# Second FFN: nine of ten blocks by seven products instead of eight, with forty plain units at five or four places of each block's steps

## The chip, the cores and the metric

The kernel runs on one core of a Trainium2 chip. The metric is the device time of one execution in microseconds (us). Three executions of the kernel before took 2602.81, 2605.07 and 2609.3 us; the median is 2605.07 us.

## The reference

One layer of a diffusion backbone with 256 context and 256 latent tokens of width 2048: a half-step SwiGLU FFN, a mixer (attention beside a bidirectional mLSTM), and a second half-step SwiGLU FFN, each behind an RMS norm with modulation by a condition vector. The change is in the second FFN, which works on the 256 latent tokens alone:

```python
def half_step_ffn(x, mod, i, g, w_up, w_down):
    h = adaln(x, g, mod, i)
    a, b = jnp.split(h @ w_up, 2, axis=-1)
    return x + 0.5 * mod[:, i + 2, None, :] * ((jax.nn.silu(a) * b) @ w_down)
...
        xl = half_step_ffn(xl, mod_l, 6, g_norm[l, 2], w_ffn2_up[l], w_ffn2_down[l])
...
    return rms_norm(xl, g_final)
```

`h` is 256 x 2048, `w_up` 2048 x 11264 (a half of 5632 columns for `a` and one for `b`), `w_down` 5632 x 2048, all in float32.

## The kernel before, in words

**Precision.** A float32 operand is split into a high part `hi` (written by ACT, line 127, rounded to the matmul's format) and the rest `lo` (by DVE, line 128). A product is made of three matmuls, hi x hi, hi x lo and lo x hi (`mm3`, lines 149 to 151). `split` does this for a weight tile of 128 x 2048 (1 MB) in two halves of 1024 columns; the `hi` and `lo` halves lie in four slots each, so a split can run at most four halves ahead of TensorE. `load_split` loads a tile into one of three `raw` slots through SP's queue (line 142) and splits it.

**Blocks.** The 5632 hidden columns are 44 groups of 128, and the second FFN takes them as eleven blocks of 512, numbers 0 to 10. Block 0 is made ahead, in the stage before. For each other block, the kernel multiplies the tokens by the block's 512 columns of `a` and of `b` (the up product), gates (`silu(a) * b`), turns the result by transposes on TensorE so that hidden columns lie on the partitions, splits it (`turned`, lines 2041 to 2062), and multiplies by the block's 512 rows of `w_down` into an accumulator `acc2`.

**Two ways to make an up product.** `up(n)` is the plain one: eight units, each loads one 1 MB tile and runs 4 x 2 x 3 = 24 matmuls of 128 x 128 by 128 x 512 (four chunks of 128 features, two halves of the tokens). `quad(n)` is a scheme with seven products in place of eight: tokens are cut in two halves and features in two halves, and the two weight halves of `a` and the two of `b` are the four parts of the other factor. Seven combinations of the token quarters (`a11`, `a12`, `a21`, `a22` and the sums `n1`, `s4`, `s2`, `s3`, built once by `token_forms`) are multiplied with seven combinations of the weight parts. Products are called m0 to m6 here, after the loop variable in `quad`; each is two steps (`q` = 0 and 1), and a step splits one 1 MB weight tile and runs 12 matmuls, into the PSUM tile X or Y. Fourteen steps have 168 matmuls, where eight plain units have 192.

**How the weight combinations come about.** Two pairs of 1 MB tiles, `weights[0]` (tags `c0` and `c1`, called chain in the profile) and `weights[1]` (called ra) change roles from block to block: one is `chain_`, the other `ra`. `chain_` is loaded plainly by SP while the block before runs (`again`, in m5, line 2121); after the split of m0 POOL adds the next part of the weights onto it with an accumulating DMA (`accum`, line 730, called by `first`), for m2; after the split of m2 DVE adds the `ra` tile to it (`summed_half`, line 2077), for m4; after the split of m4 a further accumulating DMA (`chained(0, 2)`), for m6. `ra` is loaded plainly in m0 (line 2130), read in m3, and takes an accumulating DMA for m5. m1 reads a plain load into a `raw` slot (`plain`, line 2125). Each accumulating DMA waits for the `lo` part of the split before it, on POOL's queue, and the split of the later product waits for its landing. A block by seven products so has six plain and six accumulating loads of 1 MB, a plain one eight plain loads.

**The order.** `sequence` (lines 2241 to 2249) names the order of two streams: "s" is a step of the blocks by seven products, in the order of `QUADS`; "u" is a plain unit, in the order of `units`. Plain units are the eight of an `up(n)`, and those of the down products: `down(n, n + 1)` runs eight units, each with one 1 MB load (line 142) and 24 matmuls, and adds the pair's result to `acc2`. Behind the two steps of m0 no unit stands; behind m1 to m6 one stands each, save behind m3 in the fourth and the eighth block of `QUADS`. After each "s" or "u" `turned` is called, which turns the next finished block half in the order of the block numbers; it needs one of three hid tiles (`N_HID`), which come free when a pair's down product is summed. After the sequence come the tail: `down(8, 9)` and block 10's down product with the final gate, residual and norm. `before_final` loads the gate and the final gain into the tags `c0` and `c1`, the tiles of `weights[0]`.

The program's text gives priorities and dependencies; a planner writes the list of each engine and each DMA queue from them, in order of its own estimate of when an instruction can run. An engine runs its list in order.

## Time and profile before

| | us |
|---|---|
| median of three executions | 2605.07 |
| lowest, highest | 2602.81, 2609.3 |
| the profiled execution's own time | 2604.58 |
| its span in the profile | 2602.7 |
| second FFN's sequence of steps and units, from the first plain unit to the tail | 1949.61 to 2525.90 of the span |
| tail (down products of blocks 8 to 10, norm, output) | 2525.90 to 2602.70 of the span |

The profile is of one execution. PE is TensorE's matmuls, PEld its weight loads, DVE the vector engine, ACT the scalar engine, POOL the GpSimd engine (here it issues accumulating DMAs), SP the engine that issues plain DMAs. Matmuls overlap one another, so the duration in a matmul's row (0.39 us) is longer than the distance to the next one's start. In a row of a single instruction the columns are its start, its duration, engine, line, operation, the tiles it writes and reads, and in brackets the engine's idle time before it and what ended it. For a DMA issue, the duration is that of issuing; the time to landing is told by the view of DMA issues. `hi<-raw`, `hi<-chain` and `hi<-ra` are splits of a raw slot and of the two pairs of weight tiles.

### The profile page before, as it was taken

The page shows a single profiled execution, that of the slowest core. Times are in us where ns is not written, and L with a number is a line of the kernel's source. Part 1 is how long each engine was busy: PE and PEld are TensorE (multiplying, and loading weights), DVE is VectorE, ACT ScalarE, POOL GpSimd, SP SyncE. Part 2 cuts the span into 40 slices and gives each one's busy share as a digit, 9 for nine tenths or more (in the row PEclk, how much of TensorE's full clock was granted, in tenths as well). Part 3 has the DMA queues.
Part 4 walks back from the last instruction along what each step waited for, and adds up shares of the span by engine and source line. Part 5 has one row for each costly group of instructions (what it writes and reads, how often), then busy time and mean ns, then how long its engine had stood idle before and what let it go on. Part 6 is the DMA issues. An engine that isn't in the chain of part 4 may idle for free.

```text
span 2602.7 us, 33781 instructions
## 1 busy us (share of the span) xinstructions
PE 2575.7 (99%) x12670; PEld 2144.7 (82%) x12670; DVE 2170.6 (83%) x2864; ACT 1417.7 (54%) x1810; POOL 220.7 (8%) x269
## 2 busy tenths in 40 slices
PE   8999999999999999999999999999999999999998
PEld 5788888888888888888889889888897888888887
DVE  7788888878888788888887889798889878887887
ACT  4454444544444565444454347456476676666664
POOL 0000000100000100000110000120000000000001
PEclk8999999999999999999999999999999999999999
DMA  9889999999999988889987887776768988999876
GB/s 392 350 217 265 276 277 271 262 273 285 261 287 265 278 247 240 218 215 228 225 253 266 296 312 247 242 273 213 267 239 240 269 269 260 272 273 279 256 231 176
DMA packets 127219, 681.01 MB, mean 262 GB/s; under 512 B 14152, under 2 KB 16712, under 8 KB 64976
## 3 DMA queue, kind: packets, MB, share of 16 engines
q1 hardware_dynamic: 98544, 493.25, 50.7%
q0 software_dynamic: 28512, 185.61, 36.4%
q8 instruction: 99, 1.62, 0.2%
q14 instruction: 64, 0.52, 0.1%
HBM read 660.91 MB, written 17.89 MB: 261 GB/s over the span
## 4 chain that ended last, share of the span: by engine, by line
PE 85%; DVE 7%; DMA 5%; issue 2%; ACT 1%; POOL 0%; ACTq 0%; POOLq 0%; SPq 0%; DVEq 0%
PE mm L151 21%; PE mm L150 21%; PE mm L149 21%; DVE lo L128 2%; PE mm L87 2%; PE Y L149 2%; PE Y L151 2%; PE Y L150 2%; PE X L151 2%; PE X L150 2%; PE X L149 2%; PE tr L150 1%; PE tr L149 1%; PE tr L151 1%; PE tr L87 1%
## 5 line engine op out<-in xcount | busy, mean ns | idle before, releaser
L127 ACT ACTIVATE hi<-raw 128x1024 fp32r<-128x1024 f32 (+2 forms) x500 | 517.8, 1041 | 421.1 <-PE mm L151 264.1
L128 DVE TENSOR_TENSOR lo<-raw,hi 128x1024 fp32r<-128x1024 f32 (+2 forms) x488 | 583.6, 1207 | 149.7 <-ACT hi L127 130.5
L127 ACT ACTIVATE hi<-chain 128x1024 fp32r<-128x1024 f32 x336 | 355.0, 1059 | 305.7 <-PE mm L151 188.0
L128 DVE TENSOR_TENSOR lo<-chain,hi 128x1024 fp32r<-128x1024 f32 x336 | 407.2, 1221 | 118.0 <-ACT hi L127 114.3
L149 PE MATMUL mm<-hi,hhi 128*128 128x512 f32 (+3 forms) x1024 | 393.6, 385 | 0.0
L151 PE MATMUL mm<-hi,hlo 128*128 128x512 f32 (+3 forms) x1024 | 386.7, 378 | 0.0
L150 PE MATMUL mm<-lo,hhi 128*128 128x512 f32 (+3 forms) x1024 | 386.7, 378 | 0.0
L207 DVE SCALAR_TENSOR_TENSOR junk<-sraw,cBh 128x1024 fp8e5<-128x1024 f32 x192 | 234.3, 1220 | 19.2 <-DMA sraw<-in_w_mt 16.7
L151 PEld LDWEIGHTS mm<-hi,hlo 128*128 128x128 f32 x1024 | 192.5, 188 | 33.9
L149 PEld LDWEIGHTS mm<-hi,hhi 128*128 128x128 f32 x1024 | 192.6, 188 | 31.0
L150 PEld LDWEIGHTS mm<-lo,hhi 128*128 128x128 f32 x1024 | 192.8, 188 | 30.7
L128 DVE TENSOR_TENSOR lo<-ra,hi 128x1024 fp32r<-128x1024 f32 x96 | 117.0, 1223 | 39.7 <-ACT hi L127 35.8
L127 ACT ACTIVATE hi<-ra 128x1024 fp32r<-128x1024 f32 x96 | 101.9, 1061 | 65.1 <-PE mm L151 48.4
L149 PE MATMUL mm<-hi,hid2h 128*128 128x512 f32 x352 | 137.1, 390 | 0.0
L151 PE MATMUL mm<-hi,hid2l 128*128 128x512 f32 x352 | 137.0, 389 | 0.0
L150 PE MATMUL mm<-lo,hid2h 128*128 128x512 f32 x352 | 136.9, 389 | 0.0
L207 DVE SCALAR_TENSOR_TENSOR sr<-sr,cBl 128x1024 f32<-128x1024 f32 x84 | 103.0, 1234 | 14.7 <-DMA sr<-in_w_mt 13.8
L730 POOL DMA_DIRECT2D chain<-in_w_up1b x60 | 53.1, 886 | 726.0 <-DVE lo L128 648.9
L149 PE MATMUL mm<-hhi,hi 128*128 128x512 f32 (+1 forms) x288 | 101.4, 352 | 0.0
L151 PE MATMUL mm<-hhi,lo 128*128 128x512 f32 (+1 forms) x288 | 99.0, 344 | 0.0
L150 PE MATMUL mm<-hlo,hi 128*128 128x512 f32 (+1 forms) x288 | 98.7, 343 | 0.0
L149 PE MATMUL mm<-hi,sumshl 128*128 128x512 f32 x200 | 77.8, 389 | 0.0
(517 smaller groups left out, 5650.3 us busy)
## 6 DMA issues: line engine op xcount, KB each, us to landing
raw<-in_w_dn SPq DMA_DIRECT2D x70, 1024.0 KB, 7.5
chain<-in_w_up1b POOLq DMA_DIRECT2D x60, 1024.0 KB, 9.8
sraw<-in_w_mt SPq DMA_DIRECT2D x96, 512.0 KB, 7.8
sr<-in_w_mt SPq DMA_DIRECT2D x81, 512.0 KB, 5.5
raw<-in_w_up1b SPq DMA_DIRECT2D x40, 1024.0 KB, 7.9
mraw<-in_w_m SPq DMA_DIRECT2D x32, 1024.0 KB, 7.4
raw<-in_w_up2b SPq DMA_DIRECT2D x32, 1024.0 KB, 9.9
chain<-in_w_dn POOLq DMA_DIRECT2D x30, 1024.0 KB, 8.6
```

The costliest lines, as they stand in the source:

```text
L87: ins = getattr(self.engine, name)(*a, **k)
L127: scalar[0].activation(hi, src, AF.Copy)
L128: vector[0].tensor_tensor(lo, src, hi.bitcast(F32), op=ALU.subtract)
L149: tensor[0].matmul(out_ap, sh, mh, start=first, stop=False, skip_group_check=skip)
L150: tensor[0].matmul(out_ap, sh, ml, start=False, stop=False, skip_group_check=skip)
L151: tensor[0].matmul(out_ap, sl, mh, start=False, stop=last, skip_group_check=skip)
L207: ins = nc.vector.scalar_tensor_tensor(junk() if junk else raw, raw, 1.0, cB[s], op0=ALU.mult, op1=ALU.mult, accum_out=mT[:, i, s, kt, h : ...
L730: accum = lambda dst, src: nc.gpsimd.dma_start(dst, src, accum_op=ALU.add)
```

## The change

- Block 3 is made by seven products too, so `QUADS` holds blocks 1 to 9: nine blocks, 126 steps. Only block 10 has a plain up product.
- Block 10's eight units come first in `units` (block 3's did), and the four pairs of down products (0 1, 2 3, 4 5, 6 7) follow one another.
- There are 40 plain units in place of 48: two ahead of the first step, then in the first two blocks one each behind m1, m2, m3, m4 and m6, in the seven others one each behind m1, m2, m4 and m6. No unit stands behind m5 any more, and none behind m3 from the third block on.
- With nine blocks the last one has `weights[0]` in the role `chain_`; with eight it had `weights[1]`.

The numbers computed are the same sums in another order for block 3.

```diff
@@ -1982,7 +1982,7 @@
         LAST = NF // FB - 1
-        QUADS = tuple(n for n in range(1, LAST) if n != 3)
+        QUADS = tuple(range(1, LAST))
...
@@ -2232,11 +2232,9 @@
         def units():
-            yield from up(3)
-            for n in (0, 2, 4):
+            yield from up(LAST)
+            for n in (0, 2, 4, 6):
                 yield from down(n, n + 1)
-            yield from up(LAST)
-            yield from down(6, 7)
 
         def sequence():
...
@@ -2245,7 +2243,7 @@
                 yield from "ss"
                 for m in range(1, 7):
                     yield from "ss"
-                    if m != 3 or n % 4 != 3:
+                    if m in (1, 2, 4, 6) or m == 3 and n < 2:
                         yield "u"
```

## The prediction

> **What bounds the kernel now.** I read the busy times first, then the table by stretches for the second FFN alone, then the waits of each engine there, and at the end single instructions around one product. In the table the columns after the stretch are its length and the busy time (with count) of PE, PEld, DVE, ACT and POOL, the granted clock, the DMA share and GB/s.

> ```profile
> span 2602.7 us, 33781 instructions
> PE 2575.7 (99%) x12670; PEld 2144.7 (82%) x12670; DVE 2170.6 (83%) x2864; ACT 1417.7 (54%) x1810; POOL 220.7 (8%) x269
> ```
> ```profile
> core 0: us, PE busy (x) PEld busy (x) DVE busy (x) ACT busy (x) POOL busy (x), PEclk, DMA share, GB/s
> 2002.00:2525.00 523.00, 523.00 (x2339) 432.84 (x2338) 434.74 (x411) 347.19 (x364) 37.55 (x44) 1.00 0.90 265
> 2179.08:2245.35 66.27, 66.27 (x299) 54.85 (x298) 57.08 (x56) 44.44 (x47) 5.23 (x6) 1.00 0.91 269
> 2245.35:2317.06 71.71, 71.71 (x323) 59.36 (x322) 60.52 (x59) 46.68 (x49) 5.24 (x6) 1.00 0.89 264
> ```

> The reader is to see that from 2002 to 2525 us TensorE is never idle, at full clock: the time of this stage is the sum of its matmuls. The last two rows are two blocks made by seven products, from the first matmul of one block to that of the next. The first is the fourth such block, whose third place (behind product m3) has no plain unit, so it holds five units; the second holds six. They differ by 71.71 - 66.27 = 5.44 us, one unit of 24 matmuls. A step has 12 matmuls, half of it: 2.72 us.

> **The matmuls.** The change turns one plain block (8 units) into a ninth block by seven products (14 steps): 14 x 2.72 - 8 x 5.44 = 38.08 - 43.52 = -5.44 us. Transposes, activations and adds of a block stay as many. This is all that TensorE can give, so 2604.58 - 5.44 = 2599.1 us is the floor while it stays the bound.

> **The work beside it.** A block with four units needs 66.27 - 5.44 = 60.83 us of TensorE. DVE does 57.08 us in the five-unit block and a unit is worth 60.52 - 57.08 = 3.44, so 53.6 of 60.8 us (88%); ACT 44.44 - 2.24 = 42.2 (69%). Both fit. For the transfers, these are the shares of the 16 DMA engines in that five-unit block:

> ```profile
> q0 software_dynamic: 862, 6.28, 48.4%
> q1 hardware_dynamic: 1581, 11.52, 42.3%
> ```

> Queue q0 carries the six accumulating loads that POOL issues (1.049 MB each), q1 the eleven plain ones of SP. So an accumulating load holds the engines for 0.484 x 66.27 / 6 = 5.35 us and a plain one for 0.423 x 66.27 / 11 = 2.55 us. A four-unit block moves six and ten: 32.1 + 25.5 = 57.6 us of 60.8, 95%. In sum it fits, but hardly; what decides is when each transfer is due.

> [...]

> **The transfer that comes late.** The weight tiles of a block are turned from one form to the next in place. Product m6 reads what POOL's accumulate, issued when the split of m4 is done, has made of the chain tile. Between m4 and m6 lie now a unit, m5's two steps and another unit; the change takes the unit behind m5 away in all blocks, and the one behind m3 from the third block on. The fourth block of today (above) lacks the unit behind m3 already, so up to the end of m5 it is the changed kernel's block. Its accumulates, two for m5 (chain) and two for m6 (ra), with start, duration, and what POOL waited for; then the time from issue to landing of the first, third and fourth:

> ```profile
> 2205.23 0.87 POOL L730 DMA_DIRECT2D chain<-in_w_up2b  x1 [22.30 <-DVE lo L128]
> 2209.72 0.87 POOL L730 DMA_DIRECT2D chain<-in_w_up2b  x1 [3.62 <-DVE lo L128]
> 2212.07 0.89 POOL L730 DMA_DIRECT2D ra<-in_w_up2b  x1 [1.49 <-DVE lo L128]
> 2215.27 0.88 POOL L730 DMA_DIRECT2D ra<-in_w_up2b  x1 [2.31 <-DVE lo L128]
> ```
> ```profile
> chain<-in_w_up2b POOLq DMA_DIRECT2D x1, 1024.0 KB, 8.1
> ...
> ra<-in_w_up2b POOLq DMA_DIRECT2D x1, 1024.0 KB, 13.5
> ...
> ra<-in_w_up2b POOLq DMA_DIRECT2D x1, 1024.0 KB, 17.4
> ```

> Four accumulates are asked for within 10 us and need 4 x 5.35 = 21.4 us. The last lands at 2215.27 + 17.4 = 2232.67. What it feeds, on ACT, DVE and PE (the first matmul of m6's second step):

> ```profile
> 2232.81 2.13 ACT L127 ACTIVATE hi<-ra 128x1024 fp32r<-128x1024 f32 x2 [2.24 <-DMA ra<-in_w_up2b]
> ...
> 2233.91 1.23 DVE L128 TENSOR_TENSOR lo<-ra,hi 128x1024 fp32r<-128x1024 f32 x1 [2.12 <-ACT hi L127]
> ...
> 2236.83 0.39 PE L149 MATMUL Y<-hi,h2hi 128*128 128x512 f32 x1
> ```

> ACT has waited 2.24 us for that landing; the halves are ready at 2233.91 + 1.23 = 2235.14 (2.47 us after the landing), and TensorE comes to them at 2236.83. So 1.69 us are to spare. Without the unit behind m5 TensorE comes at 2236.83 - 5.44 = 2231.39 and waits 2235.14 - 2231.39 = 3.75 us. Does the landing move as well? These are SP's issues in the same stretch, then the shares of the queues at 2206 to 2220 (first row) and 2220 to 2232 (last two):

> ```profile
> 2217.16 0.33 SPq L2125 DMA_DIRECT2D raw<-in_w_up2b  x1
> 2220.22 5.39 SPq L2121 DMA_DIRECT2D chain<-in_w_up2b  x2
> 2228.01 0.33 SPq L2125 DMA_DIRECT2D raw<-in_w_up2b  x1
> ```
> ```profile
> q0 software_dynamic: 352, 2.62, 96.5%
> ...
> q0 software_dynamic: 223, 1.57, 64.0%
> q1 hardware_dynamic: 227, 1.73, 37.0%
> ```

> While plain loads are pending the accumulates get 64% instead of 96%. The plain load of 2217 is issued when the unit behind m4 has been split, the two of 2220 when m5 has: all stay. Only that of 2228, released by the unit behind m5, goes, and it stands behind the others in SP's queue. So I keep the landing. The ends: if no plain load took a share, the four would land 8.1 us after the first issue and 5.35 apart, the last at 2229.4, and the wait would be 0.5 us; with one plain load more ahead of it, 3.75 + 2.55 = 6.3 us. I take 3.75, since the row is the very pattern. It counts in the third to eighth block: 6 x 3.75 = 22.5 us.

> The first, second and last block, each with m6's last accumulate, its landing and the matmul it feeds:

> ```profile
> 2004.37 0.86 POOL L730 DMA_DIRECT2D chain<-in_w_up2b  x1 [2.33 <-DVE lo L128]
> 2075.81 0.89 POOL L730 DMA_DIRECT2D ra<-in_w_up2b  x1 [4.09 <-DVE lo L128]
> ...
> 2496.67 0.87 POOL L730 DMA_DIRECT2D ra<-in_w_up2b  x1 [2.33 <-DVE lo L128]
> ```
> ```profile
> chain<-in_w_up2b POOLq DMA_DIRECT2D x1, 1024.0 KB, 16.8
> ra<-in_w_up2b POOLq DMA_DIRECT2D x1, 1024.0 KB, 14.3
> ...
> ra<-in_w_up2b POOLq DMA_DIRECT2D x1, 1024.0 KB, 16.1
> ```
> ```profile
> 2026.15 0.39 PE L149 MATMUL Y<-hi,h2hi 128*128 128x512 f32 x1
> ...
> 2097.86 0.39 PE L149 MATMUL Y<-hi,h2hi 128*128 128x512 f32 x1
> ...
> 2517.74 0.39 PE L149 MATMUL Y<-hi,h2hi 128*128 128x512 f32 x1
> ```

> Landing plus 2.47 against matmul minus 5.44: first 2023.64 against 2020.71, a wait of 2.9; second 2092.58 against 2092.42, 0.2; last 2515.24 against 2512.30, 2.9. A late m6 shifts the whole next block and is not made up, for within a block nothing else waits.

> **What else moves.** Block 10's eight plain loads pass from the end of SP's order to its start, in place of block 3's; its two gated tiles stay in their slots until the end, where no one else asks for them. With nine blocks the last one chains in tiles c0 and c1, so the loads of the final gate and gain wait for its m6, not its m5:

> ```profile
> 2501.62 0.33 SPq L2254 DMA_DIRECT2D g<-mod  x1
> 2507.06 0.33 SPq L2255 DMA_DIRECT2D gf<-in_g_final  x1
> ...
> 2537.00 0.69 DVE L1029 SCALAR_TENSOR_TENSOR acc<-acc,g 128x512 f32<-128x512 f32 x1
> ```

> The gate is asked for at 2501.62 and first used at 2537.00. Some 10 us later (two steps and the unit, 10.9) leaves over 20 us for one load of 2.55; what SP issues behind is the third tail load, due two units later still. I cost it at nothing; a tail load late by its own 2.55 is the upper end.

> **Sum.** 2604.58 - 5.44 + 22.5 + 2.9 + 0.2 + 2.9 = 2627.6 us against the profiled execution, 0.5 more against the median of 2605.07: 2628. With the ends of the wait (0.5, then none in the other three; 6.3, with 2.55 more in each of those) 2602 and 2651.

> **Rivals.** (1) *The cover holds.* The planner issues m6's unit ahead of m6's second step, or the burst drains faster, and only matmuls count: 2599 to 2608. For it: the lists are rewritten by the planner, and TensorE was idle nowhere in 523 us. Against it: ACT stood 2.24 us for that landing without another split put ahead. [...] (2) *A second transfer is late too*: the accumulate between m0 and m2, behind a backlog left by the late m6.

> ```profile
> 2243.01 0.87 POOL L730 DMA_DIRECT2D chain<-in_w_up2b  x1 [26.86 <-DVE lo L128]
> ...
> chain<-in_w_up2b POOLq DMA_DIRECT2D x1, 1024.0 KB, 9.5
> ...
> 2255.20 1.06 ACT L127 ACTIVATE hi<-chain 128x1024 fp32r<-128x1024 f32 x1 [0.29 <-PE Y L151]
> ```

> It lands at 2252.5, 2.7 us before its use. Two plain loads ahead of it (5.1 us) would make it 2.4 late, in eight blocks 19 us more: 2647. Against it: the block lengthens to 64.6 us and leaves the DMA engines 7 us idle. (3) *Faster than now by more than can be told*: start-up stalls of the first block would have to go too, beyond the 5.44; nothing in the change does that.

> **Chances.** The late m6 as sized: 0.55, own range 2613 to 2639 (2 to 5 us a block). Rival 1: 0.25. Rival 2: 0.17, 2640 to 2660. Rival 3: 0.03. A measurement of this kernel tells about 0.3% (7.8 us) from no change, so rival 1 is "the same", the first and rival 2 "slower". The range 2600 to 2648 leaves out the bottom of rival 1 and half of rival 2.

> **What would show it.** Blocks of about 64.6 us in place of 60.8; TensorE waiting for DVE's lo at m6's second step, ACT before it for the DMA, some 6 us; DMA share near 0.89 (57.6 of 64.6); no wait at m2, m3 or m5. Blocks of 60.8 us would prove me wrong, and so would the last accumulate landing under 13 us after issue.

## The result and the profile after

The changed kernel takes 2648.28 us (median of 2644.95 to 2650.72) beside 2605.78 us for the kernel before on the same chip: a ratio of 1.0159, with a 95% interval of 1.0144 to 1.0174. It is slower by some 42 us. The profiled execution took 2644.95 us, 40.4 more than the profiled one of before (2604.58).

The head of the page of the changed kernel: span, then TensorE, its weight loads, DVE, ACT and POOL with busy time, share and count.

```profile
span 2643.1 us, 33802 instructions
...
PE 2589.1 (98%) x12646; PEld 2148.6 (81%) x12646; DVE 2186.3 (83%) x2884; ACT 1428.1 (54%) x1826; POOL 223.9 (8%) x275
```

TensorE is busy 2589.1 us, 13.4 more than before (2575.7), although the change takes 24 matmuls away (12670 before, 12646 now). So there are two losses: time in which it is idle, and time in which the same matmuls last longer. The table by stretches of the changed kernel shows both: the whole sequence of blocks, then the third and the fifth block, from the first matmul of one to that of the next. The columns are those of the table in the prediction.

```profile
core 0: us, PE busy (x) PEld busy (x) DVE busy (x) ACT busy (x) POOL busy (x), PEclk, DMA share, GB/s
2000.00:2571.00 571.00, 542.89 (x2345) 442.05 (x2345) 455.81 (x436) 360.34 (x384) 42.64 (x49) 0.97 0.88 252
2097.62:2164.15 66.53, 62.52 (x272) 50.93 (x270) 51.15 (x48) 43.30 (x48) 5.22 (x6) 0.97 0.89 254
2232.00:2299.77 67.77, 63.87 (x271) 51.79 (x270) 53.62 (x52) 41.24 (x44) 5.23 (x6) 0.95 0.87 249
```

In 571 us TensorE is idle for 571.00 - 542.89 = 28.1 us, and the granted clock is 0.97: 3% of 571 us is 17.1 us. Before, the same table showed no idle time and 1.00. The sum is 2604.58 - 5.44 (fewer matmuls) + 28.1 + 17.1 = 2644.3 us, against the 2644.95 of the profiled execution. The two terms overlap somewhat, since TensorE also stood idle in some of the slow stretches (1.43 us of the 6.80 from 2219.20 below), so that the sum closes to 0.7 us is partly luck; the run `fill` below puts the slow clock at 15.6 us in another way. A block takes 66.5 to 67.8 us in place of the 60.83 us of its matmuls.

Where TensorE is idle, and what released it, in the same stretch (total, times, longest):

```profile
PE Y L149 <- ACT hi L127: 21.9, 8, 3.4
PE Y L150 <- DVE lo L128: 6.2, 9, 0.8
```

These are all its waits there: 28.1 us, at m6 in eight of the nine blocks (in one of them at both of its steps). ACT's waits for transfers of weights, in the same stretch (not each of them held TensorE up):

```profile
ACT hi L127 <- DMA chain<-in_w_up2b: 30.7, 8, 5.5
...
ACT hi L127 <- DMA ra<-in_w_up2b: 21.4, 5, 5.8
```

One instance, in the third block. First POOL's issues of the four accumulating loads (two for m5, two for m6), then the time from issue to landing of the third and of the last, then ACT, DVE and PE at m6's second step:

```profile
2123.76 0.86 POOL L730 DMA_DIRECT2D ra<-in_w_up2b  x1 [21.74 <-DVE lo L128]
2128.37 0.88 POOL L730 DMA_DIRECT2D ra<-in_w_up2b  x1 [3.74 <-DVE lo L128]
2130.63 0.87 POOL L730 DMA_DIRECT2D chain<-in_w_up2b  x1 [1.39 <-DVE lo L128]
2133.81 0.86 POOL L730 DMA_DIRECT2D chain<-in_w_up2b  x1 [2.30 <-DVE lo L128]
```
```profile
chain<-in_w_up2b POOLq DMA_DIRECT2D x1, 1024.0 KB, 13.7
...
chain<-in_w_up2b POOLq DMA_DIRECT2D x1, 1024.0 KB, 17.9
```
```profile
2151.77 2.00 ACT L127 ACTIVATE hi<-chain 128x1024 fp32r<-128x1024 f32 x2 [5.28 <-DMA chain<-in_w_up2b]
...
2152.86 1.23 DVE L128 TENSOR_TENSOR lo<-chain,hi 128x1024 fp32r<-128x1024 f32 x1 [4.92 <-ACT hi L127]
...
2149.24 0.39 PE L151 MATMUL Y<-hi,h2lo 128*128 128x512 f32 x1
2152.88 0.50 PE L149 MATMUL Y<-hi,h2hi 128*128 128x512 f32 x1 [3.25 <-ACT hi L127]
2154.14 0.61 PE L150 MATMUL Y<-lo,h2hi 128*128 128x512 f32 x1 [0.76 <-DVE lo L128]
2154.55 0.63 PE L151 MATMUL Y<-hi,h2lo 128*128 128x512 f32 x1
2154.98 0.63 PE L149 MATMUL Y<-hi,h2hi 128*128 128x512 f32 x1
```

The last accumulate is issued at 2133.81 and lands 17.9 us later, at 2151.7; ACT splits it at once; TensorE, done with m6's first step, stands 3.25 us for `hi` and 0.76 us for `lo`. The rows behind that show the second loss: matmuls follow one another at 0.43 us (2154.55, 2154.98) where they had followed at 0.23 us. The granted clock around this place, then at three other m6, from the table by stretches of the changed kernel:

```profile
2140.00:2149.30 9.30, 9.30 (x43) 7.54 (x41) 4.81 (x4) 4.13 (x4) 0.00 (x0) 1.00 1.03 277
2149.30:2152.88 3.58, 0.33 (x3) 0.00 (x1) 0.02 (x1) 1.11 (x2) 0.00 (x0) 1.00 0.95 391
2152.88:2158.35 5.47, 4.71 (x13) 3.49 (x13) 5.47 (x6) 4.44 (x5) 0.00 (x0) 0.69 0.86 328
2158.35:2170.00 11.65, 11.65 (x57) 9.61 (x56) 9.07 (x10) 8.84 (x11) 1.74 (x2) 1.00 0.98 250
```
```profile
2021.20:2024.60 3.40, 3.17 (x8) 2.52 (x9) 3.40 (x5) 2.93 (x4) 0.00 (x0) 0.51 1.05 414
2219.20:2226.00 6.80, 5.37 (x12) 3.90 (x13) 5.86 (x6) 5.41 (x6) 0.00 (x0) 0.50 0.83 336
2287.50:2294.30 6.80, 6.33 (x14) 4.67 (x15) 6.79 (x7) 4.88 (x6) 0.00 (x0) 0.50 0.86 341
```

After the wait the clock is at half (0.50 and 0.51 in the three rows) for a stretch of some 3.4 or 6.8 us, then full again. The trace's clock records have eight such stretches, one behind the wait of each of eight blocks (all but the second, which has no wait), and none in the sequence of the kernel before.

### The profile page after: what moved, and what is told of

Its sections match the earlier page's. It is cut to its first block, busy times and chain, and to the rows that moved or that the text cites. A ratio compares the mean times of both kernels' runs of the same rounds, so it can differ in the third digit from the quotient of the medians.

```text
span 2643.1 us, 33802 instructions
## 1 busy us (share of the span) xinstructions
PE 2589.1 (98%) x12646; PEld 2148.6 (81%) x12646; DVE 2186.3 (83%) x2884; ACT 1428.1 (54%) x1826; POOL 223.9 (8%) x275
## 4 chain that ended last, share of the span: by engine, by line
PE 81%; DMA 8%; DVE 6%; issue 3%; ACT 1%; POOL 0%; ACTq 0%; POOLq 0%; DVEq 0%
PE mm L149 20%; PE mm L151 20%; PE mm L150 20%; DMA chain<-in_w_up2b 4%; DVE lo L128 3%; PE mm L87 2%; PE Y L150 2%; PE Y L151 2%; PE Y L149 2%; PE tr L150 2%; PE tr L151 2%; PE tr L149 2%; DMA ra<-in_w_up2b 1%; PE tr L87 1%; ACT hi L127 1%
## 5 line engine op out<-in xcount | busy, mean ns | idle before, releaser
L127 ACT ACTIVATE hi<-raw 128x1024 fp32r<-128x1024 f32 (+2 forms) x488 | 504.6, 1040 | 411.4 <-PE mm L151 267.0
L128 DVE TENSOR_TENSOR lo<-raw,hi 128x1024 fp32r<-128x1024 f32 (+2 forms) x476 | 568.4, 1209 | 140.4 <-ACT hi L127 125.4
L127 ACT ACTIVATE hi<-chain 128x1024 fp32r<-128x1024 f32 x352 | 371.1, 1059 | 334.3 <-PE mm L151 185.3
L128 DVE TENSOR_TENSOR lo<-chain,hi 128x1024 fp32r<-128x1024 f32 x352 | 426.2, 1222 | 132.2 <-ACT hi L127 128.9
L149 PE MATMUL mm<-hi,hhi 128*128 128x512 f32 (+3 forms) x1024 | 393.6, 385 | 0.0
L151 PE MATMUL mm<-hi,hlo 128*128 128x512 f32 (+3 forms) x1024 | 386.8, 378 | 0.0
L151 PEld LDWEIGHTS mm<-hi,hlo 128*128 128x128 f32 x1024 | 192.5, 188 | 33.9
L149 PEld LDWEIGHTS mm<-hi,hhi 128*128 128x128 f32 x1024 | 192.6, 188 | 31.1
L128 DVE TENSOR_TENSOR lo<-ra,hi 128x1024 fp32r<-128x1024 f32 x104 | 126.7, 1223 | 52.4 <-ACT hi L127 50.4
L127 ACT ACTIVATE hi<-ra 128x1024 fp32r<-128x1024 f32 x104 | 109.7, 1060 | 85.0 <-PE mm L151 41.5
L149 PE MATMUL mm<-hi,hid2h 128*128 128x512 f32 x352 | 137.7, 391 | 0.0
L151 PE MATMUL mm<-hi,hid2l 128*128 128x512 f32 x352 | 137.0, 389 | 0.0
L730 POOL DMA_DIRECT2D chain<-in_w_up1b x60 | 53.0, 884 | 727.5 <-DVE lo L128 674.6
L149 PE MATMUL mm<-hhi,hi 128*128 128x512 f32 (+1 forms) x288 | 101.4, 352 | 0.0
L151 PE MATMUL mm<-hhi,lo 128*128 128x512 f32 (+1 forms) x288 | 99.0, 344 | 0.0
L149 PE MATMUL Y<-hi,h2hi 128*128 128x512 f32 x144 | 62.5, 434 | 21.9 <-ACT hi L127 21.9
## 6 DMA issues: line engine op xcount, KB each, us to landing
raw<-in_w_dn SPq DMA_DIRECT2D x70, 1024.0 KB, 7.3
chain<-in_w_up1b POOLq DMA_DIRECT2D x60, 1024.0 KB, 10.4
raw<-in_w_up1b SPq DMA_DIRECT2D x40, 1024.0 KB, 8.2
mraw<-in_w_m SPq DMA_DIRECT2D x32, 1024.0 KB, 7.4
chain<-in_w_dn POOLq DMA_DIRECT2D x30, 1024.0 KB, 9.1
chain<-in_w_up2b POOLq DMA_DIRECT2D x28, 1024.0 KB, 9.7
```

The lines of the kernel that those rows point to most:

```text
L127: scalar[0].activation(hi, src, AF.Copy)
L128: vector[0].tensor_tensor(lo, src, hi.bitcast(F32), op=ALU.subtract)
L149: tensor[0].matmul(out_ap, sh, mh, start=first, stop=False, skip_group_check=skip)
L151: tensor[0].matmul(out_ap, sl, mh, start=False, stop=last, skip_group_check=skip)
L730: accum = lambda dst, src: nc.gpsimd.dma_start(dst, src, accum_op=ALU.add)
```

## The experiments

The theory: m6's last accumulating load is late since no unit stands behind m5; TensorE waits for it in nearly every block; and each wait halves the clock for a while, which adds to its price. The rivals: the ninth block itself (another order of loads, other tiles in the tail), the four accumulates beside the plain loads of the next block, or DVE. Seven kernels take these apart, and two try to mend what was found. A ratio is to the kernel before on the same chip.

**The places alone, the ninth block kept: `places_1245`.** The unit behind m6 goes back behind m5.

```diff
-                    if m in (1, 2, 4, 6) or m == 3 and n < 2:
+                    if m in (1, 2, 4, 5) or m == 3 and n < 2:
```

> Nine blocks as changed, but each block's four units stand behind m1, m2, m4 and m5 (and m3 in the first two), not m6. Theory (late accumulate, then half clock): m6's last accumulate gets 5.44 us more time, against some 4.4 us by which TensorE waits for it now, so the waits at m6 go, the clock stays at 1.0 and the time is 2599 to 2606 us. Rival (the blocks ask for more of the DMA engines than 60.8 us hold, 95% on the mean): the same work in the same number of units, so the waits only move to another product and the time stays above 2630 us.

It took 2614.27 us, ratio 1.0036 (1.0022 to 1.0049), above the 2599 to 2606 expected: some 33 us of the loss are gone by one place, but 15 us stay above the floor of the prediction. Its table by stretches and TensorE's waits from 2005 to 2560:

```profile
2005.00:2560.00 555.00, 545.48 (x2416) 443.96 (x2415) 466.16 (x450) 364.62 (x390) 44.40 (x51) 1.00 0.91 266
```
```profile
PE Y L150 <- DVE lo L128: 5.6, 10, 0.8
PE tr L2055 <- DVE ca L2078: 3.3, 4, 1.0
```

No wait is longer than 1.0 us, and the clock is 1.00. TensorE is idle 9.5 us, in short pieces: at m2, at m6, and where a block begins (there its transposes wait for a product of DVE). With m6 early, other transfers have no time to spare, such as m2's accumulate (in the third block ACT stood 3.82 us for it). The rest of the 15 us stands in TensorE's busy time, 2575.2 us on the page, 4.9 more than 2575.7 - 5.44; what makes it was not followed up. So a unit behind m5 takes the long wait away, but with the four units at these places other due times are missed by a little.

**The places alone, without the ninth block: `eight_moved`.** The sequence of before with its eight blocks; the units behind m3, m5 and m6 all stand behind m6.

```diff
                 for m in range(1, 7):
                     yield from "ss"
-                    if m != 3 or n % 4 != 3:
+                    if m in (1, 2, 4):
                         yield "u"
+                yield from "uu" if n % 4 == 3 else "uuu"
```

> The kernel before, eight blocks and 48 units, but the units behind m3, m5 and m6 all stand behind m6. Only places change, no matmul, no load. Theory: without units behind m3 and m5 the last accumulate of m6 is late by about 4.4 us in each of eight blocks and the clock halves after it (2 us more): 40 to 55 us slower than before, 2645 to 2660 us. Rival (it is the ninth block's added loads): no more loads than before, so 2605 us, no change.

It took 2649.85 us, ratio 1.0165 (1.0147 to 1.0183), with as many matmuls as before. TensorE's waits from 2005 to 2560:

```profile
PE Y L149 <- ACT hi L127: 18.2, 8, 3.2
PE Y L150 <- DVE lo L128: 6.1, 8, 0.8
```

The same wait stands in each of the eight blocks (in the profiled execution, the fastest of four, the clock fell behind three of them). Neither the ninth block nor the smaller number of units is needed for it: a block with as many units as before, but none between m5 and m6, has it too.

**The idle time filled: `fill`.** Sixteen further matmuls stand behind m6's first step, into a PSUM tile that nobody reads. At 0.227 us each (a unit's 5.44 us over 24 matmuls) they are 3.63 us a block. They move no data and make nothing early; they only keep TensorE at work through the wait.

```diff
                         mm3(B[dst], a[0][:, k, :], a[1][:, k, :], *wt(slice(j * CB, (j + 1) * CB)), fresh and k == 0, k == 7, True)
+                    if (m, q) == (6, 0):
+                        tb = tbank()
+                        for _ in range(16):
+                            nc.tensor.matmul(tb, a[0][:, 3, :], wt(slice(3 * CB, 4 * CB))[0], start=True, stop=True, skip_group_check=True)
```

> The changed kernel with 16 matmuls more in each block, behind m6's first step, on data already there, into a PSUM tile that nobody reads: 3.63 us of TensorE work in the place of the wait. Theory (the wait stays, the half clock after it is a matter of TensorE's idleness): the clock stays at 1.0 at m6, the 17 us of slow matmuls go, 2628 to 2634 us. Rival (the clock drops for another reason, or the second step is slow because its tile comes late in pieces): 2645 us or more, with the 0.43 us spacing still there.

It took 2638.82 us, ratio 1.0127 (1.0112 to 1.0143): some 9 us less than the changed kernel, with 9 x 3.63 = 32.7 us more matmuls. From 2005 to 2560:

```profile
2005.00:2560.00 555.00, 551.66 (x2454) 452.98 (x2453) 449.53 (x431) 355.76 (x379) 41.76 (x48) 1.00 0.89 258
```

The clock is 1.00 throughout. The time of before less 5.44, plus 32.7 of filler, plus the 555.00 - 551.66 = 3.3 us of idle time that remain, makes 2635.1, against 2637.30 for the profiled execution; some 2 us are open. It lies above the 2628 to 2634 expected, since filler and remaining idle time are 36.0 us where the waits were 28.1: the filler stands in the second block too, which had no wait, and short waits are left behind it. That the clock falls because of the idle time is thereby shown: with TensorE kept at work, no stretch of the sequence ran at half clock. The price follows too: the profiled execution is 7.65 us shorter than the changed kernel's, with 7.9 us more of filler and idle time, so the half clock had cost some 15.6 us.

**The plain loads of the next block, later: `again_m6`.** The two loads that `again` issues stand in m6 in the text, not in m5.

```diff
-                (s3, lambda q: ra[q], "X", False, again, c22),
-                (a22, held, "Y", True, None, c21),
+                (s3, lambda q: ra[q], "X", False, None, c22),
+                (a22, held, "Y", True, again, c21),
```

> The changed kernel, but the two plain loads for the next block (issued in m5 and pending beside m6's accumulates) are issued in m6. Theory (plain loads take 36% of the engines from the accumulates from the middle of the burst on): the last accumulate lands up to 3 us earlier, TensorE waits 1 to 2.5 us instead of 4.4 per block, mostly short of the drop of the clock: 2605 to 2625 us. Rival (accumulates alone fill the burst, plain loads matter little): landing at 17 us as now, 2645 us; or the next block's m0 now waits for its load and takes the gain back.

2646.65 us, ratio 1.0157 (1.0141 to 1.0172). It tells nothing: in its trace these loads are issued where they were (at 2138.82 us in the third block, 2138.76 in the changed kernel), since their tile is free once m5 is split. The next run asks the same in another way.

**The plain loads of the next block, all but gone: `again_short`.** They bring 128 of 2048 columns.

```diff
-                    nc.sync.dma_start(ra[q], part(QUADS[i + 1], 0, q))
+                    nc.sync.dma_start(ra[q][:, :128], part(QUADS[i + 1], 0, q)[:, :128])
```

> The changed kernel, but the two plain loads for the next block, pending beside m6's accumulates, fetch only 128 of 2048 columns (the rest of the weight tile is left as it was, so the output is not the reference's). The loads in the text's order could not be moved, since the planner issues them when their tile is free. Theory that the prediction went by (plain loads take up to 36% from the accumulates in the second half of the burst): about 3 us less of them before the last landing, so it lands 2 to 3 us earlier, TensorE waits 1.5 to 2.5 us in place of 4.4, the clock mostly stays up: 2610 to 2628 us. Rival (the four accumulates alone make the lateness): landing stays at 17 us after issue, 2640 us or more.

2633.83 us, ratio 1.0100 (1.0078 to 1.0122), between the two that were expected. TensorE's waits from 2005 to 2560:

```profile
PE Y L149 <- ACT hi L127: 13.1, 8, 2.1
PE Y L150 <- DVE lo L128: 6.1, 8, 0.8
```

In the eight blocks that wait, the last accumulate lands 15.9 to 17.0 us after its issue, where the changed kernel has 16.5 to 19.1. The wait for `hi` falls from 21.9 to 13.1 us. So these two plain loads hold the last accumulate back by about 1 us a block. The rest of the lateness is left to the four accumulating loads among themselves and the other plain loads beside them; this run does not part the two.

**The last accumulate left out: `no_last`.** The second of the two loads of `chained(0, 2)` is not issued, so m6 multiplies an incomplete weight sum.

```diff
-                (s2, held, "X", False, chained(0, 2), c12),
+                (s2, held, "X", False, lambda q: q or chained(0, 2)(q), c12),
```

> The changed kernel without m6's last accumulating load (the second of the two, in every block): that part of the weights is left out of the sum, so the output is not the reference's. Theory (this one landing is what TensorE waits for): no wait at m6's second step, the clock stays at 1.0, and nothing else becomes late, so the time is the floor of the matmuls, 2599 to 2603 us, against 2648 with it: 45 us for nine loads of 1 MB. Rival (the stage is short of DMA or DVE throughput as a whole): nine loads are 48 us of DMA engine time less, 9% of the stage's, so that the waits shrink but those at other products stay: 2610 to 2630 us.

2602.26 us, ratio 0.9978 (0.9969 to 0.9987). From 2005 to 2560:

```profile
2005.00:2560.00 555.00, 555.00 (x2484) 458.87 (x2483) 477.84 (x461) 375.21 (x397) 39.50 (x46) 1.00 0.87 255
```

TensorE is busy in all of 555.00 us. Without this one transfer the whole loss is gone. By the medians (2607.1 us for the kernel before, beside it) the change is then worth 4.8 us, by the ratio 0.22% or 5.7 us: both near the 5.44 us of the matmuls. The run also takes this load's own engine time away, so it does not tell when the load is due from what it adds to the others; `last_dve` below, which still fetches it, does more.

**What is left in `places_1245`: `p1245_short`.** The cut of `again_short` in the kernel with the units behind m1, m2, m4 and m5.

> Units behind m1, m2, m4 and m5 with the same two plain loads cut to 128 columns (output not the reference's). It asks what the 14 us are that this order still loses against the floor of 2599.7: if transfers at 95% of the engines (waits at m2's and m6's accumulates), 5 us of DMA time less per block take nearly all of them: 2600 to 2605 us. If DVE, which has six steps on end without a unit between them (m6, m0, m1), they stay: 2610 to 2615 us.

2603.33 us, ratio 0.9985 (0.9975 to 0.9994). From 2005 to 2560:

```profile
2005.00:2560.00 555.00, 554.23 (x2480) 457.05 (x2479) 477.26 (x459) 376.08 (x397) 46.98 (x54) 1.00 0.88 243
```

Of 9.5 us of idle time 0.8 are left, while DVE is busier than in `places_1245` (477.26 against 466.16 us in the same 555). So the rest there is transfer time too, and not DVE.

**One accumulating load turned into a plain one: `last_dve` and `p1245_dve`.** If the accumulates are the burden, the late one can be a plain load into a raw slot, asked for a step earlier; DVE, which has room, adds it in two halves. First in the changed kernel, then in `places_1245`. The sums stay complete.

```diff
+            def fourth(q):
+                if q == 0:
+                    chained(0, 2)(0)
+                    g["r"] = raw_tile()
+                    nc.sync.dma_start(g["r"], part(n, 0, 3))
...
+                elif m == 5:
+                    w = slice(q * 1024, (q + 1) * 1024)
+                    add(chain_[1][:, w], chain_[1][:, w], g["r"][:, w])
...
-                (s2, held, "X", False, chained(0, 2), c12),
+                (s2, held, "X", False, fourth, c12),
```

> The changed kernel, but the fourth accumulating load of a block (the one that m6's second step waited for) is a plain load into a raw slot, issued a step earlier, and two half adds of VectorE at m5 put it onto the held sum; the sums are the same. By the theory (late is the accumulating load, whose 1 MB took 5.35 us beside 2.55 us for a plain one, and the idle time then halves the clock) the DMA work of a block falls by 2.8 us, nothing waits at m6 any more and no stretch runs at half clock: 2600 to 2607 us. VectorE gets 2 adds of half a tile a block (about 2.3 us of 61, to some 92 percent busy). By the rival (any burst behind m4 is late, or the raw slot that is held from m4 to m5 holds back the units' loads, or VectorE is too full) TensorE waits elsewhere and it stays above 2620 us.

> The same replacement in the kernel with the units behind m1, m2, m4 and m5 (2614.27 us, where TensorE waited 0.4 to 1.7 us a block for m2's sums and for the blocks' first steps, and where cutting the two plain loads of the next block gave 2603.33 us). If what was left there is DMA time, 2.8 us less of it a block gives 2601 to 2606 us, below the kernel before. If it is VectorE's lateness at m2, its two added half adds a block make it no faster: 2612 us or more.

`last_dve` took 2600.98 us beside 2606.66 for the kernel before: 0.9980 (0.9971 to 0.9989). It is the fastest complete kernel of this study. Its stretch from 2005 to 2560, and all of TensorE's waits there:

```profile
2005.00:2560.00 555.00, 554.47 (x2481) 458.18 (x2480) 495.60 (x476) 374.03 (x395) 39.24 (x45) 1.00 0.89 272
```
```profile
PE Y L150 <- DVE lo L128: 0.5, 1, 0.5
```

One wait of 0.5 us is left. DVE does 495.60 of 555 us where the changed kernel's does 455.81 of 571 (89 against 80%; a part of this is that the blocks follow one another faster), and the DMA share is 0.89, with 272 GB/s in place of 252. Its profiled execution took 2599.41 us; the floor of the prediction was 2599.1. With the places as the change has them, and with a plain load in place of the late accumulate, the ninth block gives what its matmuls promise. The load changes in two ways here, in kind and in being asked for a step earlier; which of them does more was not tried.

`p1245_dve` took 2606.79 us, 0.9996 (0.9987 to 1.0005), which cannot be told from the kernel before and lies just above the 2601 to 2606 expected. It is some 9 us faster than `places_1245`, each set against the kernel before on its chip; its profiled execution took 2602.61 us, and TensorE is busy 553.54 of the 555 us. Why its median lies 4 us above that was not followed up.

## Why the prediction was right in mechanism and short in size

- **The matmuls (-5.44 us): right.** `no_last` and `last_dve` are 4.8 and 5.7 us faster than the kernel before beside them, by the medians, and `last_dve` profiled at 2599.41 us where the floor was put at 2599.1.
- **The transfer that comes late: right, place and cause.** It is m6's last accumulate; it lands 17.9 us after its issue in the third block, where the row of the earlier pattern had 17.4. ACT stood 5.28 us for it (some 6 expected). `no_last` shows that without it nothing else is late, `eight_moved` that the place of the units alone makes it late. One detail was off: m6's second step waits for `hi` first (21.9 us) and then for `lo` (6.2 us), not for `lo` only.
- **The size of the waits: right.** 22.5 + 2.9 + 0.2 + 2.9 = 28.5 us were predicted and 28.1 measured; the third block waits 3.25 + 0.76 = 4.0 us where 3.75 was taken, and the second block has none where 0.2 was taken.
- **The step that failed is the price of a wait.** Under "The transfer that comes late" a wait of 3.75 us is costed at 3.75 us. Each also put TensorE at half clock for one or two stretches of 3.4 us: 15.6 to 17.1 us that stand in no term of the sum. With 17.1 the 2627.6 becomes 2644.7, against 2644.95. The own range of the late m6 (2613 to 2639) let the length of the wait vary, but nothing that follows a wait; the time lies above it, at the very end of the whole range (2648). That it came so near that end is luck: the end was worked out from longer waits (6.3 us a block, and 2.55 us more in three), and none came; the longest at m6's second step was 3.4 + 0.8 us. `fill` shows the term by itself.
- **The working beside it.** DMA share 0.89 and 0.87 a block, against 0.89 expected. Blocks of 66.5 and 67.8 us against 64.6: the difference of 2 to 3 us is the half clock.
- **The plain loads' share.** "While plain loads are pending the accumulates get 64%" made me keep the landing, and this was right; `again_short` puts the share of the next block's two plain loads at about 1 us a block.
- **Rival 1 (the cover holds)** fell: no unit was put ahead of m6's second step. TensorE is the busiest engine still, at 98% of the span, and yet some 45 us went to waiting for transfer engines that are busy 0.88 of the time, and to what followed the waits. **Rival 2 (a second transfer late too)**, at 2647 us, comes near the number by a mechanism that did not happen: no wait of the changed kernel lies at m2. In `places_1245`, where m6 comes early, m2's accumulate did become one of the next late things: TensorE waits 0.5 to 1.1 us at m2 in five of its blocks. **Rival 3** did not happen; `last_dve` shows that the floor itself is only 0.2% below the kernel before.
- **The tail's loads, costed at nothing: right.** In the changed kernel's trace TensorE has no wait from 2571 us to its end.

## What to carry to other kernels

Work taken from between a transfer's issue and its use must be counted per due time, not per block: here the sum of transfers fitted (57.6 of 60.8 us), and one of them was late in nearly every block. Where the wait that follows is on TensorE (2.3 us in all in the first block here, 4.0 in the third), ask whether the clock falls after it, and price it with that; here the loss came to 1.6 times the wait itself (45.2 us for 28.1). The cure that worked best here was to change the late transfer (a plain load, asked for earlier, and an add on an engine with room) and not the places of the units.

## What the runs showed of the hardware that was not expected

The clock fell after waits that were far from long. In the first block of the changed kernel TensorE waited 1.57 us and then 0.76 us, and ran one matmul between; these are the stretch that holds the two waits and the one behind it:

```profile
2017.80:2021.20 3.40, 1.30 (x5) 0.52 (x3) 1.05 (x1) 2.14 (x3) 0.00 (x0) 1.00 0.96 405
...
2024.60:2030.00 5.40, 5.40 (x25) 4.49 (x24) 4.64 (x6) 3.24 (x4) 0.86 (x1) 0.99 0.87 272
```

```profile
2352.34:2355.75 3.41, 1.68 (x8) 1.04 (x6) 0.00 (x0) 0.00 (x0) 0.00 (x0) 1.00 1.00 416
2355.75:2359.16 3.41, 1.07 (x4) 0.67 (x5) 1.84 (x3) 2.93 (x3) 0.00 (x0) 1.00 0.88 372
2488.88:2492.28 3.40, 1.63 (x6) 1.12 (x7) 2.41 (x3) 3.40 (x5) 0.00 (x0) 1.00 1.01 426
```
```profile
2094.36:2097.77 3.41, 1.71 (x8) 1.09 (x6) 0.00 (x0) 0.38 (x1) 0.00 (x0) 1.00 0.96 360
2097.77:2101.19 3.42, 1.93 (x7) 1.23 (x7) 2.71 (x3) 3.42 (x5) 0.00 (x0) 1.00 1.00 424
```

Behind the first of them (TensorE busy 1.68 of 3.41 us, 49%) the clock stayed full; behind the second (31%) and the third (48%) it fell to 0.50. In `eight_moved` it stayed full behind both (50 and 56%; 1.00 from 2100 to 2200), though TensorE stood idle for 2.44 + 0.76 = 3.2 us in all across them, longer than the 1.57 + 0.76 us of the first block above. In the 3.41 us ahead of each of the eight falls in the changed kernel's trace TensorE worked 0.02 to 1.63 us. So the length of a wait alone did not tell here whether the clock fell; that it matters how a wait lies to these stretches is the author's estimate from the rows above, and no run was made for it. In the changed kernel's trace the clock fell in each of the eight blocks that wait, in that of `eight_moved` in three of eight.

An accumulating load of 1 MB took the DMA engines about twice as long as a plain one (5.35 against 2.55 us in the prediction's rows). The changed kernel's third block, with six accumulating and ten plain loads in 66.53 us, says the same, 5.48 against 2.63 us:

```profile
q0 software_dynamic: 869, 6.33, 49.4%
q1 hardware_dynamic: 1443, 10.49, 39.6%
```

`last_dve` agrees: one of six accumulating loads a block turned into a plain one took nearly all the waits away, with as many bytes fetched.
